# Mixed tile order, sample units dealt out by work, interleaved value products and earlier page loads in a decoder step

## The chip, the cores and the metric

The kernel runs on one core of a Trainium2 chip, as one program launched once. The metric is the device time of one execution in microseconds (us). The core has five engines with a queue each: TensorE (PE, matmuls; its weight loads are shown apart as PEld), VectorE (DVE), ScalarE (ACT), GpSimd (POOL) and SyncE (SP), which here only issues DMAs. Each engine takes its instructions in the order in which they were put down when the program was built, and semaphores make one wait for another.

## The reference

One layer of a hybrid decoder is computed for a prompt of 1024 rows and for a sample group of 8 sequences with 4 rows each, 1056 rows in all, with a width of 1024 and all arithmetic in float32:

- RMS norm with a shift and a scale from a conditioning vector, then one combined projection into gate inputs u and v, 8 query heads, six key/value parts, branch gates and merge gates;
- mixer A: v is normalised, mixed in time within chunks of 128 rows by a lower-triangular matrix, and multiplied by u;
- mixer B: attention with three branches. Compressed: each block of 64 rows is pressed by a small two-layer network into one key and one value, and a softmax goes over these. Selected: a softmax over the 16 best blocks of 64 rows. Window: a softmax over the last 512 rows. Sigmoid gates weigh and add the three;
- both mixers go through a projection, are gated, added, projected and added to x;
- a feed-forward part with a causal convolution of width 3, and a last RMS norm.

The sample sequences have a past of 8192 rows each, in 64 pages of 128 rows that a page table names. The compressed branch reads all pages' compression rows, and the selected branch's keys and values lie in the same pages:

```python
kc = compress_blocks(rows[:, :, :, 0], cmp_pe[0], cmp_w1[0], ...)
p_cmp = masked_softmax(jnp.einsum('btkgd,bnkd->btkgn', qg, kc), avail)
_, sel_idx = lax.top_k(imp, n_sel)
s = jnp.einsum('qkgd,qksid->qkgsi', qi, kg)
...
s = jnp.einsum('bnqkgd,bnjkd->bnqkgj', qg, kw[:, :, :, 0])
o_win = jnp.einsum('bnqkgj,bnjkd->bnqkgd', p, kw[:, :, :, 1])
```

## The kernel before

The program is written stage by stage. A recording layer gives each instruction its place in its engine's queue: it goes through the program with estimated durations and lets an instruction that is ready go ahead of an earlier one that is not. So the order in a queue is near the order of the code but not the same, and it is fixed once the program is built.

Projections are kept feature by row: 128 features by 1056 rows in three column pieces of 384, 384 and 288 (`products`, line 396). Each float32 product is made of three matmuls on a high and a low part of its operands. All matmuls but transposes go through the helper `mm` on line 55, so the profile shows most of them under that line. `slot()` hands out one of 24 buffers of 128 by 1056; PSUM tiles come from four small pools (`pA` with 3 banks for scores, `pT`, `pO`, `pU`).

The compression of the sample pages is cut into 16 parts (`compress`, line 517, and `compress_end`, line 531). Part n loads 32 page tiles of 128 KB into one buffer, does 64 matmuls on it, then an activation and two small products. There is one such buffer, and from part 9 on a second one for odd parts, so the pages of the next part can be loaded when the matmuls of the last one in that buffer are done. `load_pages` (line 491) issues the loads in groups of four; of eight groups in a row it gives those numbered 1, 4 and 6 to ScalarE's queue and the others to SP's. The parts are dealt over the projections: parts 5 to 8 lie behind the four u projections, parts 9 to 13 behind groups of four further projections, and parts 14 and 15 come after the last merge gates, the loads of the queries and the building of key tiles (`key_tiles`, line 733).

The attention stage holds two kinds of work that have nothing to do with each other until its end:

- 32 prompt units: 8 tiles of 128 query rows, each with 4 pairs of heads. `attend` (line 1054) makes scores, maxima, exponentials and scalings of a unit; `combine` (line 1112) transposes the probabilities and multiplies them by the values, two units later (`AHEAD`). Tile i sees i + 1 key tiles in the selected branch and up to 5 in the window branch, so a unit of tile 7 has several times the work of one of tile 0. At the start of a tile `qtile` (line 1004) makes its split queries and the compressed branch.
- the sample group: two windows (`sample_window`, line 861), each for four sequences; 32 sample units, a quarter of a sequence's selected pages each, with scores (`sel_scores`), a transposition called the turn (`sel_turn`) and value products (`sel_values`); after each fourth unit a merge (`sel_merge`). A unit loads 16 page tiles of 128 KB into one of four buffers, which it shares with the windows and with eight late chunks of the conditioning product (`ada_late`).

The loop at line 1162 deals the second kind over the first: iteration n attends unit n, combines unit n - 2 and does sample unit n - 2. The tiles run in the order of `TILES` on line 24.

In a sample window the value products multiply, for each of four sequences i, four pieces k of 128 window rows, and a last piece with the four new rows. The output of sequence i goes to partitions 32i to 32i + 31, that is to the i-th group of 32 columns of TensorE's array; the profile shows such a matmul as 128*32 (rows by columns of the stationary tile).

Of the kernel before, what the change touches and what calls it, by code (L numbers as in the profile page):

```python
# [20 lines left out]
AHEAD = 2  # L21
S2, S3 = 4, 2
EARLY = 8
TILES = (0, 1, 2, 3, 4, 5, 6, 7)
YP = (0, 1, 3, 5, 7), (2, 5)
VD = (0, 2, 4, 6, 8)
SCALE = {1: "dppd", 2: "ppddppdd"}
# [22 lines left out]
def step_kernel(tc, A):  # L50
# [3 lines left out]
    def mm(out, lhsT, rhs, start, stop):  # L54
        return pe.matmul(out, lhsT, rhs, start=start, stop=stop)  # L55
# [17 lines left out]
    def pU():  # L73
        return psum([128, 512], F32, "U", 2)
# [440 lines left out]

    hidden = {}

    def compress(n):
        b, half = n // 2, n % 2
        home = "b" if n >= LATE and n % 2 else "a"  # L520
        st = (R2B if home == "b" else PG)([128, 32, 256], F32, "st", 1)
        load_pages([(st[:, i], A["pcmp"], b * 64 + half * 32 + i) for i in range(32)], freed.get(home))
        ps = pU()
        for d in range(32):
            for s in range(2):
                mm(ps[64 * s:64 * s + 64, 0:128], w1(d, s),
                   st[:, :, s * 128 + 4 * d:s * 128 + 4 * d + 4], d == 0, d == 31)
        hidden[n] = ps, home
# [194 lines left out]
    for n in range(9, 14):  # L723
        for _ in range(4):
            next(fill)()
        compress(n)
        compress_end(n)
    for f in fill:
        f()
    for b in range(8):  # L730
# [130 lines left out]
    def sample_window(gr):  # L861
# [30 lines left out]
        pe.transpose(pt[0:32, 0:128], s[:, 512:544], ident)  # L892
        dve.tensor_copy(pst[0:32, 512:640], pt[0:32, 0:128])
        po = pU()
        for i in range(4):
            v = wv[:, i]
            for k in range(4):
                mm(po[32 * i:32 * i + 32, 0:128], pst[:, 128 * k + 32 * i:128 * k + 32 * i + 32], v[:, k], k == 0, False)
            mm(po[32 * i:32 * i + 32, 0:128], pst[0:32, 512 + 32 * i:544 + 32 * i], vs_new[:, 128:256], False, True)
        ow = R3([128, 128], F32, "ou", 5)  # L900
        uses[use] = act.copy(ow, po[:, 0:128])
# [247 lines left out]
    def sel_first(m):  # L1149
        if 0 < m <= 32:  # L1150
            turned[m - 1] = sel_turn(m - 1, held[m - 1][2])
        if 0 <= m < 32:
            held[m] = sel_scores(m)

    def sel_second(m):
        if 0 < m <= 32:
            use, st, _ = held.pop(m - 1)
            sel_values(m - 1, use, st, turned.pop(m - 1))
            if m % 4 == 0:
                sel_merge(m // 4 - 1)  # L1160

    for n in range(len(units) + AHEAD + 1):
        attend_n(n)
        if n < 2:
            sample_window(n)
        sel_first(n - 2)
        combine_n(n - AHEAD)
        sel_second(n - 2)
        if n % 4 == 1 and n < 32:
            ada_late()  # L1170

# [337 lines left out]
```

## Time and profile before

| what | value |
|---|---|
| time, median of 3 runs | 2093.46 us (2092.12 to 2093.72) |
| the profiled execution's own time | 2091.29 us |
| its span in the trace | 2089.4 us |
| TensorE busy | 1984.5 us, 95% |
| VectorE busy | 992.5 us, 48% |
| ScalarE busy | 748.0 us, 36% |
| GpSimd busy | 314.6 us, 15% |
| read from HBM | 264.57 MB |

The busy times say how long an engine had something in work, not whether it worked at its best. TensorE's clock has two levels, 2.4 and 1.2 GHz, and the profile gives the granted share of it for each stretch: 1.00 is the upper level throughout, 0.50 the lower. Where one matmul of a group goes through other columns of the array than the next one, their records lie over each other in time, so a group's length is read from the first start to the last end.

### The profile page before, as it was taken

To read this page: it belongs to the slowest core of one execution; us is meant where nothing else is said; L and a number is where in the kernel's file an instruction comes from. 1 tells how busy PE (TensorE), PEld (TensorE's weight loads), DVE (VectorE), ACT (ScalarE), POOL (GpSimd) and SP (SyncE) were. 2 spreads that over 40 slices of the span, in tenths; PEclk is the share of its full clock that TensorE was granted. 3 is DMA by queue.
4 is the path that set the end of the run, shared out by engine and by line. 5 is a ranking of instruction groups with operands and counts; after the bars stand their busy time and mean duration, and the time that the engine had idled before them with its cause. 6 is when DMAs were issued, how large, how long until landed. Compare 5 with 4: busy or idle time off the path is not lost.

```text
span 2089.4 us, 41176 instructions
## 1 busy us (share of the span) xinstructions
PE 1984.5 (95%) x15449; PEld 1813.2 (87%) x15449; DVE 992.5 (48%) x2273; ACT 748.0 (36%) x1598; POOL 314.6 (15%) x506
## 2 busy tenths in 40 slices
PE   5889899999998999999999999999999999999996
PEld 3889899999996566666669999999999999999995
DVE  6512521111125476667663767545353453453466
ACT  3311211212123455556562356541331422413433
POOL 3410010100001132222330500210110100101102
PEclk7999999999996899999999999999999999999998
DMA  8465577655464787757531634121221111111112
GB/s 309 137 201 156 180 223 249 218 163 163 144 221 145 222 254 244 256 155 240 166 107 65 237 116 141 52 70 56 66 66 46 45 47 46 46 46 46 40 50 84
DMA packets 217671, 288.35 MB, mean 138 GB/s; under 512 B 25504, under 2 KB 170048, under 8 KB 215296
## 3 DMA queue, kind: packets, MB, share of 16 engines
q1 hardware_dynamic: 155152, 207.88, 31.0%
q10 hardware_dynamic: 57040, 59.58, 9.0%
q0 software_dynamic: 5280, 18.26, 2.4%
q8 instruction: 122, 2.00, 0.4%
q14 instruction: 77, 0.63, 0.1%
HBM read 264.57 MB, written 25.21 MB: 139 GB/s over the span
## 4 chain that ended last, share of the span: by engine, by line
PE 85%; DVE 7%; DMA 4%; ACT 2%; issue 1%; SPq 1%; ACTq 0%; DVEq 0%
PE t L55 81%; PE t L1122 3%; DMA t<-pcmp 2%; DVE t L1085 1%; PE t L939 1%; DMA t<-psel 1%; DVE t L1110 1%; SPq L512 1%; DVE t L1394 1%; DVE t L307 1%; DVE t L766 0%; DMA t<-xT 0%; DMA t<-w_bb 0%; ACT t L306 0%; DVE t L1253 0%
## 5 line engine op out<-in xcount | busy, mean ns | idle before, releaser
L55 PE MATMUL t<-t,t 128*128 128x384 f32 (+12 forms) x14738 | 1899.9, 319 | 72.7 <-DVE t L159 14.7
L55 PEld LDWEIGHTS t<-t,t 128*128 128x128 f32 (+2 forms) x14610 | 1729.8, 169 | 194.2 <-issue 92.2
L307 DVE TENSOR_TENSOR t<-t,t 128x512 fp32r<-128x512 f32 (+5 forms) x322 | 240.8, 755 | 439.3 <-ACT t L306 436.2
L306 ACT CAST t<-t 128x512 fp32r<-128x512 f32 (+5 forms) x322 | 205.2, 646 | 421.2 <-PE t L55 311.4
L1110 POOL TENSOR_SCALAR t<-t,t 128x384 f32<-128x384 f32 (+3 forms) x96 | 118.5, 1247 | 356.5 <-DVE t L1104 94.5
L1237 DVE SCALAR_TENSOR_TENSOR t<-t,t,t 128x384 f32<-128x384 f32 (+1 forms) x168 | 95.9, 572 | 111.0 <-PE t L55 110.3
L1086 ACT ACTIVATE t<-t,t 128x384 f32<-128x384 f32 (+3 forms) x192 | 105.7, 554 | 55.3 <-DVE t L1085 30.5
L1085 DVE TENSOR_REDUCE t<-t 128x1 f32<-128x384 f32 (+3 forms) x192 | 96.6, 516 | 46.9 <-PE t L55 45.7
L1306 ACT COPY t<-t 128x384 f32<-128x384 f32 x132 | 58.6, 444 | 142.1 <-PE t L55 142.1
L1125 ACT COPY t<-t 128x512 f32<-128x512 f32 (+1 forms) x136 | 76.7, 575 | 56.4 <-PE t L1122 46.3
L1122 PE MATMUL t<-t,t 128*128 128x128 f32 x528 | 90.2, 293 | 0.0
L1315 POOL COPY t<-t 128x2 f32<-128x2 f32 x44 | 19.0, 431 | 435.4 <-ACT t L1306 435.4
L1320 DVE SCALAR_TENSOR_TENSOR t<-t,t,t 128x1072 f32<-128x1072 f32 x44 | 58.7, 1335 | 53.6 <-ACT t L1319 53.6
L1122 PEld LDWEIGHTS t<-t,t 128*128 128x128 f32 x528 | 59.7, 146 | 27.0 <-issue 22.6
L662 ACT ACTIVATE t<-t 128x384 f32<-128x384 f32 (+1 forms) x48 | 22.3, 465 | 133.1 <-PE t L55 98.4
L1319 ACT ACTIVATE t<-t,t 128x1072 f32<-128x1072 f32 x44 | 56.5, 1285 | 28.6 <-DVE t L1308 27.7
L1321 DVE SCALAR_TENSOR_TENSOR t<-t,t,t 128x1072 f32<-128x1072 f32 x44 | 58.7, 1334 | 1.4
L539 DVE TENSOR_SCALAR t<-t,t 128x64 f32<-128x64 f32 x16 | 4.5, 283 | 95.0 <-PE t L55 94.8
L1110 DVE TENSOR_SCALAR t<-t,t 128x384 f32<-128x384 f32 (+3 forms) x96 | 48.9, 562 | 0.3
L534 ACT ACTIVATE t<-t,t 128x128 f32<-128x128 f32 x16 | 7.8, 490 | 101.8 <-PE t L55 96.4
L1300 POOL MEMSET t<- 128x2 f32 x44 | 4.3, 99 | 253.7 <-DVE t L1321 156.1
L1225 POOL TENSOR_TENSOR t<-t,t 128x384 f32<-128x384 f32 (+1 forms) x24 | 28.0, 1173 | 83.2 <-DVE t L1224 81.1
(259 smaller groups left out, 963.9 us busy)
## 6 DMA issues: line engine op xcount, KB each, us to landing
t<-psel SPq DMA_DIRECT2D x384, 128.0 KB
t<-pcmp SPq DMA_DIRECT2D x320, 128.0 KB
t<-pcmp ACTq DMA_DIRECT2D x192, 128.0 KB
t<-w_up SPq DMA_DIRECT2D x88, 256.0 KB
t<-psel ACTq DMA_DIRECT2D x128, 128.0 KB
t<-w_ada SPq DMA_DIRECT2D x16, 1024.0 KB
t<-t SPq DMA_DIRECT2D x28, 528.0 KB
t<-w_t ACTq DMA_DIRECT2D x52, 256.0 KB
```

The source lines that it names most:

```text
L55: return pe.matmul(out, lhsT, rhs, start=start, stop=stop)
L306: act.copy(hi, t)
L307: dve.tensor_tensor(lo, t, hi.bitcast(F32), op=OP.subtract)
L1085: dve.tensor_reduce(nm, bk, axis=AX.X, op=OP.max, negate=True)
L1086: act.activation(P[:, w:w + n], bk, AF.Exp, bias=nm, accum_out=s8[:, branch, h, c:c + 1])
L1110: (dve if e == "d" else pool).tensor_scalar(P, P, fc, None, op0=OP.mult)
L1122: pe.transpose(pt[:, 256 * a + 128 * h:256 * a + 128 * h + 128], P[:, c:c + 128], ident)
L1125: act.copy(pp[:, 0:n], pt[:, 0:n])
L1237: dve.scalar_tensor_tensor(x[:, a:e], ps[:, 0:e - a], gate[:, f, 0:1], base[:, a:e], op0=OP.mult, op1=OP.add)
L1306: act.copy(up[:, 2 + a:2 + e], ps[:, 0:e - a])
L1320: dve.scalar_tensor_tensor(acc[:, 0:w], up[:, 1:1 + w], cw[:, n, 1:2], acc[:, 0:w], op0=OP.mult, op1=OP.add)
L1321: dve.scalar_tensor_tensor(acc[:, 0:w], up[:, 2:2 + w], cw[:, n, 2:3], acc[:, 0:w], op0=OP.mult, op1=OP.add)
```

## The change

Five things are altered.

- The order of the prompt's tiles becomes 4, 5, 1, 6, 0, 7, 2, 3.
- Each prompt unit gets a weight, `i + 1 + min(i + 1, 5) + 6` for tile i. The 33 sample steps are dealt to the iterations in proportion to the summed weights; none to the first two, and three to the third. An iteration can have no sample step, one or several. Of several, the first unit's scores come ahead of the combination, the others behind it.
- In a sample window the value products run over the pieces k outside and the sequences i inside, with the four products of the new rows at the end.
- The page loads of compression parts 14 and 15 are written ahead of the last merge gates and of the key tiles, in a function `compress_load` of their own.
- The page loads of part 5 all go to SP's queue.

```diff
-TILES = (0, 1, 2, 3, 4, 5, 6, 7)
+TILES = (4, 5, 1, 6, 0, 7, 2, 3)
...
+    paged = {}
+
+    def compress_load(n):
         b, half = n // 2, n % 2
         home = "b" if n >= LATE and n % 2 else "a"
         st = (R2B if home == "b" else PG)([128, 32, 256], F32, "st", 1)
-        load_pages([(st[:, i], A["pcmp"], b * 64 + half * 32 + i) for i in range(32)], freed.get(home))
+        load_pages([(st[:, i], A["pcmp"], b * 64 + half * 32 + i) for i in range(32)], freed.get(home),
+                   () if n == 5 else (1, 4, 6))
+        paged[n] = st, home
+
+    def compress(n):
+        if n not in paged:
+            compress_load(n)
+        st, home = paged.pop(n)
...
+    for n in (14, 15):
+        compress_load(n)
     for f in fill:
         f()
...
         po = pU()
+        for k in range(4):
+            for i in range(4):
+                mm(po[32 * i:32 * i + 32, 0:128], pst[:, 128 * k + 32 * i:128 * k + 32 * i + 32], wv[:, i, k], k == 0, False)
         for i in range(4):
-            v = wv[:, i]
-            for k in range(4):
-                mm(po[32 * i:32 * i + 32, 0:128], pst[:, 128 * k + 32 * i:128 * k + 32 * i + 32], v[:, k], k == 0, False)
             mm(po[32 * i:32 * i + 32, 0:128], pst[0:32, 512 + 32 * i:544 + 32 * i], vs_new[:, 128:256], False, True)
...
+    work = [i + 1 + min(i + 1, 5) + 6 for i, _ in units]
+    due = [33 * sum(work[0:n + 1]) // sum(work) for n in range(len(units))] + [33] * (AHEAD + 1)
+    m = 0
     for n in range(len(units) + AHEAD + 1):
         attend_n(n)
         if n < 2:
             sample_window(n)
-        sel_first(n - 2)
+            due[n] = 0
+        mine = range(m, due[n])
+        m = max(m, due[n])
+        for k in mine[0:1]:
+            sel_first(k)
         combine_n(n - AHEAD)
-        sel_second(n - 2)
+        for k in mine:
+            if k > mine[0]:
+                sel_first(k)
+            sel_second(k)
```

The built programs can be compared row by row; such a row has the line, the operation, the tile written, the tiles read and the shape of what is written. Three places follow.

On TensorE, the value products of the first sample window, before. `t755_7736` is the output in PSUM, `t747_7701` holds the window's values, `t752_7726` the turned probabilities and `t171_605` the new rows:

```order
L889 MATMUL t753_7727<-t1_69,t749_7716 128x128 x4
L892 MATMUL t754_7733<-t1_69,t749_7716 32x128
L55 MATMUL t757_7759<-t1_69,t708_7571 128x128
L55 MATMUL t755_7736<-t747_7701,t752_7726 32x128 x4
L55 MATMUL t755_7736<-t171_605,t752_7726 32x128
L55 MATMUL t755_7736<-t747_7701,t752_7726 32x128 x4
L55 MATMUL t755_7736<-t171_605,t752_7726 32x128
L55 MATMUL t755_7736<-t747_7701,t752_7726 32x128 x4
L55 MATMUL t755_7736<-t171_605,t752_7726 32x128
L55 MATMUL t755_7736<-t747_7701,t752_7726 32x128 x4
L55 MATMUL t755_7736<-t171_605,t752_7726 32x128
L55 MATMUL t768_7799<-t769_7800,t413_4101 32x512 x4
```

The same place in the changed program, where the tiles have other numbers:

```order
L900 MATMUL t759_7759<-t1_69,t755_7748 128x128 x4
L903 MATMUL t760_7765<-t1_69,t755_7748 32x128
L55 MATMUL t763_7791<-t1_69,t708_7571 128x128
L55 MATMUL t761_7768<-t753_7733,t758_7758 32x128 x16
L55 MATMUL t761_7768<-t171_605,t758_7758 32x128 x4
L55 MATMUL t780_7863<-t781_7864,t413_4101 32x512 x4
```

The sixteen products now follow each other with the sequence changing at each step, and the four products of the new rows come behind them; what stands ahead and behind is the same.

On VectorE, the key tiles (lines 749 to 751, which are 760 to 762 in the changed program) and the two evictions of compression part 14 (lines 539 and 544, now 548 and 553), before:

```order
L749 TENSOR_TENSOR t_7091<-t_7092,t_7089 64x1024
L750 CAST t_7089<-t_7089 64x1024
L751 CAST t_7090<-t_7090 64x1024
L751 CAST t_7091<-t_7091 64x1024
L812 COPY t_7504<-t_7513 128x4
L539 TENSOR_SCALAR t_606<-t_7310,t_577 128x64
L544 TENSOR_TENSOR t_607<-t_7314,t_580 64x128
```

and in the changed program:

```order
L760 TENSOR_TENSOR t_7301<-t_7302,t_7299 64x1024
L761 CAST t_7299<-t_7299 64x1024
L823 COPY t_7504<-t_7513 128x4
L762 CAST t_7300<-t_7300 64x1024
L548 TENSOR_SCALAR t_606<-t_7415,t_577 128x64
L553 TENSOR_TENSOR t_607<-t_7419,t_580 64x128
L762 CAST t_7301<-t_7301 64x1024
```

One of the two casts of the first key tile has moved behind the evictions.

On TensorE, the first attention scores behind compression part 15 (the rows with 16 matmuls), before, with tile 0:

```order
L55 MATMUL t_7423<-t_7318,t_566 64x128 x16
L55 MATMUL t_7667<-t_7088,t_7120 128x128
L55 MATMUL t_7667<-t_7090,t_7120 128x128
L55 LDWEIGHTS t_72
L55 MATMUL t_7667<-t_76,t_72 128x128
L55 MATMUL t_7673<-t_7089,t_7120 128x128
L55 MATMUL t_7673<-t_7091,t_7120 128x128
```

and in the changed program, with tile 4:

```order
L55 MATMUL t_7423<-t_6984,t_566 64x128 x16
L55 MATMUL t_7667<-t_7298,t_7330 128x384
L55 MATMUL t_7667<-t_7300,t_7330 128x384
L55 MATMUL t_7672<-t_7298,t_7330 128x256
L55 MATMUL t_7672<-t_7300,t_7330 128x256
L55 LDWEIGHTS t_72
L55 MATMUL t_7672<-t_76,t_72 128x128
```

Each head's scores now come in two pieces of 384 and 256 columns instead of one of 128, with one mask (the product with `t_72`) for both.

## Rows read from the trace of the kernel before

**Rows 1.** From the page: the engines' totals, and two rows of the span in 40 equal slices of 52.2 us, TensorE's busy share and its granted clock, in tenths.

```profile
PE 1984.5 (95%) x15449; PEld 1813.2 (87%) x15449; DVE 992.5 (48%) x2273; ACT 748.0 (36%) x1598; POOL 314.6 (15%) x506
...
PE   5889899999998999999999999999999999999996
...
PEclk7999999999996899999999999999999999999998
```

**Rows 2.** Busy time of each engine in stretches of the attention stage: start and end in us, length, then busy us and instructions of PE, PEld, DVE, ACT and POOL, TensorE's granted clock, the DMA engines' busy share and GB/s.

```profile
637.00:668.00 31.00, 21.48 (x203) 15.92 (x202) 22.96 (x104) 14.69 (x59) 6.96 (x10) 0.69 0.65 213
668.00:698.00 30.00, 25.65 (x138) 15.09 (x138) 3.59 (x12) 2.59 (x7) 0.00 (x0) 0.63 0.30 88
698.00:800.00 102.00, 96.25 (x970) 62.41 (x971) 72.91 (x208) 57.74 (x171) 27.20 (x20) 0.95 0.82 260
800.00:915.00 115.00, 109.64 (x1118) 72.82 (x1117) 71.70 (x218) 64.22 (x190) 26.71 (x22) 0.97 0.72 224
915.00:1010.00 95.00, 94.09 (x957) 63.51 (x957) 65.88 (x190) 58.70 (x173) 29.90 (x24) 1.00 0.66 205
1010.00:1103.00 93.00, 85.41 (x829) 58.92 (x826) 61.19 (x173) 59.03 (x147) 27.76 (x20) 0.98 0.44 146
```

**Rows 3.** What TensorE waited for from 698 to 1103 us: the waiting line, what released it, us in total, number of waits, the longest. There are 13 such rows, of 19.2 us.

```profile
PE t L55 <- DVE t L985: 3.1, 3, 1.7
PE t L1029 <- DVE t L1027: 2.8, 2, 2.6
PE t L55 <- DVE t L976: 2.4, 1, 2.4
PE t L55 <- ACT t L306: 2.2, 1, 2.2
...
PE t L939 <- ACT t L932: 1.6, 3, 0.7
...
PE t L55 <- DVE t L944: 1.5, 1, 1.5
...
PE t L55 <- DMA t<-psel: 0.6, 1, 0.6
PE t L943 <- DVE t L988: 0.4, 1, 0.4
...
PE t L55 <- DVE t L929: 0.2, 1, 0.2
```

**Rows 4.** The same from 637 to 698 us, the longest row.

```profile
PE t L889 <- DVE t L885: 5.1, 2, 3.1
```

**Rows 5.** Busy time in three short stretches, columns as in rows 2: the value products of sample window 0, of window 1, and of the first sample unit.

```profile
670.79:680.23 9.44, 9.44 (x45) 5.72 (x48) 0.00 (x0) 0.00 (x0) 0.00 (x0) 0.53 0.00 0
687.18:695.37 8.19, 8.19 (x45) 5.22 (x48) 0.00 (x0) 0.00 (x0) 0.00 (x0) 0.62 0.23 65
709.54:710.60 1.06, 1.06 (x37) 0.86 (x30) 1.06 (x4) 0.91 (x4) 0.17 (x1) 1.00 0.62 193
```

**Rows 6.** TensorE's groups of matmuls by shape from 670.7 to 680.2 us: line, operation, stationary tile, moving tile, count, then busy us, mean ns of one, idle us before them.

```profile
L55 PE MATMUL t<-t,t 128*32 128x128 f32 x32 | 7.6, 420 | 0.0
L55 PE MATMUL t<-t,t 32*32 32x128 f32 x8 | 2.3, 382 | 0.0
```

**Rows 7.** VectorE's groups by shape from 636.6 to 668.3 us, columns as in rows 6 with what ended the idle time: maxima (line 1085), query differences (766), scalings (1110) and one of the two small steps (1106).

```profile
L1085 DVE TENSOR_REDUCE t<-t 128x1 f32<-128x128 f32 x16 | 4.4, 281 | 4.0 <-PE t L55 3.8
L1085 DVE TENSOR_REDUCE t<-t 128x1 f32<-128x256 f32 x7 | 2.7, 411 | 0.0
L766 DVE TENSOR_TENSOR t<-t,t 64x128 fp32r<-64x128 f32 x8 | 2.2, 286 | 0.2
L1110 DVE TENSOR_SCALAR t<-t,t 128x128 f32<-128x128 f32 x8 | 2.0, 288 | 0.0
L1106 DVE RECIPROCAL t<-t 128x4 f32<-128x4 f32 x5 | 0.9, 176 | 0.3 <-ACT t L1086 0.2
```

**Rows 8.** Groups of VectorE from 636 to 1103 us, for the wider shapes of the same lines.

```profile
L1085 DVE TENSOR_REDUCE t<-t 128x1 f32<-128x384 f32 x80 | 43.4, 550 | 13.8 <-PE t L55 13.3
...
L1110 DVE TENSOR_SCALAR t<-t,t 128x384 f32<-128x384 f32 x40 | 22.3, 590 | 0.1
...
L1110 DVE TENSOR_SCALAR t<-t,t 128x256 f32<-128x256 f32 x28 | 15.4, 563 | 0.0
```

**Rows 9.** Two stretches, columns as in rows 2: the matmuls of compression part 5, and the 72 matmuls of the last merge gate (48 of 384 columns, 24 of 288).

```profile
254.00:261.20 7.20, 7.20 (x130) 7.03 (x129) 0.00 (x0) 0.47 (x1) 0.00 (x0) 1.00 0.00 0
602.70:614.30 11.60, 11.60 (x75) 11.43 (x73) 1.07 (x3) 1.40 (x3) 0.53 (x1) 1.00 0.72 228
```

**Rows 10.** VectorE in order of time from 622 us: start, us, line, operation, shapes, count.

```profile
624.24 1.41 DVE L751 CAST t<-t 64x1024 fp32r<-64x1024 f32 x2
...
625.75 0.28 DVE L539 TENSOR_SCALAR t<-t,t 128x64 f32<-128x64 f32 x1
```

**Rows 11.** TensorE in order of time from 600 us, with the idle time before a row and what ended it in brackets.

```profile
626.09 11.09 PE L55 MATMUL t<-t,t 128*64 128x128 f32 x137 [3.49 <-DVE t L539]
```

**Rows 12.** SP's queue in order of time from 228 us: the first 14 of the 20 page loads of compression part 5 that it issues.

```profile
231.59 11.76 SPq L512 DMA_DIRECT2D t<-pcmp  x14
```

**Rows 13.** SP's queue from 212 to 219 us: the last page loads of compression part 4.

```profile
212.56 5.89 SPq L512 DMA_DIRECT2D t<-pcmp  x9
```

**Rows 14.** TensorE in order of time from 213 us.

```profile
223.05 4.14 PE L55 MATMUL t<-t,t 128*64 128x128 f32 x48 [5.51 <-DMA t<-w_t]
```

More of the change, by code (lines that the diff above doesn't have):

```diff
@@ L516, in step_kernel @@
     hidden = {}
-    def compress(n):
+    paged = {}
+    def compress_load(n):
         b, half = n // 2, n % 2
```

## The prediction

> **What bounds the kernel now.** I read the page's head first. TensorE is busy for 1984.5 of 2089.4 us, and its granted clock falls in three places only: at the start, in slices 13 and 14 of 40, which is 627 to 731 us, and a little in the last slice [rows 1]. So the kernel is bound by TensorE's work, and a change that does not alter that work can only win idle time, clock, or overlap between matmuls. The second view cuts the run into stretches [rows 2]. From 637 to 1103 us lies the attention stage that the change reorders. In 637 to 668 TensorE works 21.5 of 31 us at a granted clock of 0.69; in 668 to 698 it works 25.7 of 30 at 0.63, while VectorE does 3.6 us and ScalarE 2.6. After 698 TensorE is nearly full (96 of 102, 110 of 115, 94 of 95, 85 of 93 us). The third view, the waits, says what the rest is: after 698 thirteen kinds of wait make 19.2 us, and no kind is over 3.1 [rows 3]; before 698 the longest is for the scaling of a sample window's scores (line 885), 5.1 us in two waits [rows 4]. Every stretch outside the stage keeps its matmuls.
>
> **The change part by part.** All sums are made against the profiled execution, 2091.29 us (a span of 2089.4 with 1.9 around it), which is 2.2 under the median of the three runs.
>
> *Value products of the sample windows.* The same 40 matmul records of each window (32 with 128 rows, 8 with 32 rows) now go through the four column groups in turn instead of finishing one group first. Before, they fill 9.44 us at clock 0.53 and 8.19 us at 0.62, with VectorE and ScalarE at 0.00 in both [rows 5], so nothing runs beside them and all 17.6 us are on the path. In the first window the 32 large ones take 7.6 us and the 8 small ones 2.3 [rows 6]. A sample unit's own value products have the same shape, count and column groups, in the order that the change brings: 32 records in 1.06 us at a granted clock of 1.00 [rows 5]. At half clock that is 2.1 us. The small ones were four pairs at about 0.6 us; one batch of all four I put at 0.6. Window 0 keeps its wait and low clock ahead of it: 2.7 us. Window 1 lies between 2.7 and 1.4 (full clock); I take 2.0. Saved: 17.6 - 4.7 = 12.9 us. Bounds: 0, if the groups still queue for a reason I don't see, and 14.8, if both run at full clock. No transfer becomes late: the first unit's pages are issued before window 0, and those of the next wait for window 0's buffer and so start earlier too.
>
> *Tile 4 first.* The windows hang on a chain of small VectorE steps, and VectorE is busy 23 of 31 us in 637 to 668 [rows 2]. What stands between it and the scaling of window 0 was, by the order and [rows 7]: 16 maxima of 128 columns (4.5 us), 7 of 256 (2.9), 8 and 2 scalings (2.3 and 1.1), 10 small steps (1.8), 8 query differences (2.3): 14.9 us. Now it is 11 maxima of 256 (4.5), 12 of 384 (6.6), 4 scalings of 256 and 4 of 384 (2.3 and 2.4), 14 small steps (2.5): 18.3 [rows 7, 8]. So window 0 comes some 3.4 us later. TensorE does more meanwhile: 27 matmuls of 256 columns, 24 of 384 and 6 masks are 16,900 columns against 10,600 before, and 72 projection matmuls (25,344 columns) took 11.6 us [rows 9], so 6,300 columns are 2.9 us of work done early. I count 0 for the two together; bounds -4 (the wide units also keep the clock up) and +5 (the chain's own latency grows).
>
> *Mixed order and dealt units behind it.* Work is unchanged, so only waits and clock can go. After 698 the waits are 19.2 us; lost clock, length times (1 - granted), is 102 x 0.05 + 115 x 0.03 + 93 x 0.02 = 10.4 [rows 2, 3]. Four kinds belong to sample units and their merges (lines 985, 976, 944, 988: 7.4 us [rows 3]); in the new order merges 0 to 2 stand beside tiles 5, 5 and 6, where before they stood beside tiles 2, 3 and 4. The starts of tiles (line 1027, 2.8), the turns (939, 1.6) and the end of the stage (306, 2.2) stay as they are. I take 5 of the 7.4 and 2 of the clock: -7. Bounds: -29 (all of it) and +22 (each of 32 turns waits the 0.7 us that the longest did).
>
> *Last compression pages ahead of keys.* The loads stand in the same place in SP's and ScalarE's rows as before, since the recording layer had already put them ahead of the key loads. What moves is the two evictions of compression 14, one VectorE cast earlier in the key tiles. TensorE waited 3.49 us for the first of them (line 539), which was queued behind two casts of 0.7 us each (line 751) [rows 10, 11]: -0.7 us; bounds -1.4 and 0.
>
> *Page loads of compression 5 all on SP.* SP issues 32 loads instead of 20, with two stores among them. Compression 5 runs at 254.0 to 261.2 [rows 9], and by the order 21 projection matmuls now stand ahead of it that stood behind: 21 x 0.16 = 3.4 us, so the pages must be there by 257.4. SP alone issued 9 loads in 5.89 us, 0.65 each, the last until 218.45, and TensorE, which had waited for compression 4's pages (its 128*64 matmuls; the row names another transfer that landed with them), went on at 223.05, 4.6 us later [rows 13, 14]. From 231.6 that gives 231.6 + 32 x 0.65 + 4.6 = 257.0: in time, by 0.4 us. At the 0.84 of the stretch in which both queues issued (14 in 11.76 us [rows 12]) it would be 263, 5.7 late. I take 0, with bounds 0 and +6. The Trainium skill (DMA: Bandwidth & Descriptors, "Issuing engines are not separate DMA queues") says that transfers issued from several engines share the same 16 DMA engines, so that a second queue saves issue time alone; by that rule the slower pitch is the shared engines' and not SP's, and the cost is 0.
>
> Sum: 2091.3 - 12.9 + 0 - 7 - 0.7 + 0 = 2070.7, and 2.2 more on the scale of the median: **2073 us**.
>
> **Rivals.**
> *Only the windows pay.* The waits after 698 are spread over thirteen kinds [rows 3], which speaks for a residue that moves and doesn't shrink. 2073 + 7 = 2080.
> *The order fills everything.* Half of the 29 us instead of a quarter: 2073 - 8, and with the start's -4, 2061. For it: TensorE idles under 1 us in 915 to 1010, with wide tiles [rows 2]. Against: tile 0 and tile 1 still come, in between.
> *The clock stays low.* The clock fell while TensorE waited at 637 to 668 and came back inside the long bursts of window products (granted 0.53 and 0.62 over them [rows 5]). With bursts of 2 to 3 us between the same waits it may not come back until the first combine: window 1 at 2.7, and some 4 us of work behind it at twice the time: 2078. The Trainium skill (TensorE: Matmul & The Clock Gate, "HAM oscillation — how this bites in real kernels") tells of just this: short bursts between waits are each run at the lower rate.
> *Pages are late.* In iteration 2 three units follow each other. A unit's 16 pages are 2.1 MB, 8 us at the 260 GB/s of 698 to 800 [rows 2], and of the 405 us after 698, 12.7 per attention unit, the change's own weights give a sample unit 6 parts in 14, some 5 us of TensorE's time. Four units 3 us late each: 2085. Against: four buffers run ahead, and pages cost TensorE 0.6 us in the whole stage before [rows 3].
> *Column groups don't overlap in the windows.* 2073 + 12.9 = 2086. Against: the same shapes do in [rows 5].
> *Turns wait, and it is slower.* A unit's turn (line 939) needs add, maximum and exponential of its scores, behind a wide tile's maxima of 0.55 us each on VectorE [rows 8]. If two or three units per iteration leave too little TensorE work between scores and turn, every unit pays. From 0.65 us per unit (20.6 / 32) the gain is gone; at 0.8, 2073 + 26 = 2099. Against: three waits of 32, 1.6 us in all [rows 3].
>
> **How the numbers follow.** Forecast 0.37, only the windows 0.22, everything filled 0.12, clock low 0.09, pages late 0.09, no overlap 0.03, turns wait 0.08. A difference of 0.2% is 4.2 us, about what a measurement of this kernel can tell from no change. Faster: everything but the last, and of the two near 2085 a fifth less: 0.88; same 0.05; slower 0.07. The range leaves out the slower case and the far end of the best: 2056 to 2088.
>
> **What would show it.** Right: each window's value products in 1.4 to 3 us; the windows' end some 12 us earlier against the end of compression 15; PE's waits after it at 10 to 15 us; no wait ahead of compression 5. Wrong: windows still 8 us long; a wait on the turns or on selected pages in most units; a gap before compression 5 or 8; waits at the stage's end, where the last sample units now stand next to the release of their buffers.

## The result, and the profile after

The changed kernel takes 2080.95 us (median of 4 runs, 2079.78 to 2082.61), the kernel before 2093.59 in the same comparison (4 runs, 2092.12 to 2094.11). The ratio is 0.9941, 95% interval 0.9924 to 0.9959: the interval lies below 1, so the kernel is faster, by some 0.6%, 8 us above the forecast of 2073 and inside the range of 2056 to 2088. The number is that of the rival "only the windows pay" (2080), and the experiments had to say whether its reason holds as well. Measured again in another comparison, the kernel after ("after" from here on) stood at 0.9964 (0.9948 to 0.9981).

The page of the kernel after, with the rows that answer to [rows 1]:

```profile
PE 1966.6 (95%) x15449; PEld 1803.3 (87%) x15449; DVE 992.6 (48%) x2273; ACT 748.1 (36%) x1598; POOL 315.4 (15%) x506
...
PE   5889899999996899999989999999999999999996
...
PEclk7999999999997999999999999999999999999998
```

The matmuls are the same 15449, and TensorE is busy 17.9 us less with them: busy time holds waiting inside a column group and half clock too. In slices 13 and 14 (624 to 728 us) its share is lower than in [rows 1], 6 and 8 tenths, since the products that filled them are shorter and the waits aren't; the granted clock there is 7 and 9 tenths, where it was 6 and 8. The 8 in slice 21 (1040 to 1092 us) is new.

The stretches of the kernel after, columns as in [rows 2]: the value products of window 0 and window 1 (with the two small products ahead of each), from there to the last matmul of the stage, and from there to the first product of the next stage.

```profile
676.40:679.25 2.85, 2.84 (x46) 2.10 (x50) 0.00 (x0) 0.05 (x1) 0.00 (x0) 0.62 0.00 0
685.12:688.13 3.01, 3.00 (x46) 1.95 (x50) 0.00 (x0) 0.15 (x1) 0.00 (x0) 0.55 0.89 278
688.13:1086.80 398.67, 381.80 (x3903) 257.76 (x3902) 269.30 (x793) 237.87 (x684) 108.87 (x88) 0.98 0.67 209
1086.80:1093.38 6.58, 0.01 (x2) 0.00 (x1) 1.57 (x3) 2.68 (x4) 0.00 (x0) 0.61 1.01 403
```

And the same two last stretches in the kernel before:

```profile
695.37:1100.50 405.13, 387.56 (x3890) 258.18 (x3890) 269.60 (x785) 237.58 (x677) 111.57 (x86) 0.97 0.66 210
1100.50:1102.73 2.23, 0.03 (x2) 0.00 (x1) 2.13 (x4) 2.15 (x4) 0.00 (x0) 1.00 0.96 351
```

The rows of [rows 5] begin with the first value product. Without the two small products, which take the first 0.74 and 0.50 us, the windows' value products went from 9.44 and 8.19 us to 2.11 and 2.51. The stretch behind them is 6.5 us shorter; the idle stretch at the end of the stage is 4.4 us longer, and in it the DMA engines are full (1.01, 403 GB/s).

What TensorE waited for from 637 us to 1092 us in the kernel after (line, releaser, us, times, longest), against [rows 3] and [rows 4]:

```profile
PE t L1040 <- DVE t L1038: 6.5, 4, 2.2
PE t L55 <- ACT t L1097: 5.3, 9, 1.3
PE t L900 <- DVE t L896: 5.2, 2, 3.3
PE t L55 <- DVE t L851: 4.2, 1, 4.2
...
PE t L55 <- DVE t L996: 1.3, 1, 1.3
...
PE t L950 <- ACT t L943: 0.2, 1, 0.2
```

The wait ahead of the windows is as before (5.1, now 5.2, line 896). The sample units' merges (line 996) and turns (line 950) hardly wait any more. The starts of tiles (lines 1038 and 1040) do, four times. The wait of 4.2 us is for line 851, in the selection of the sample group's blocks ahead of the windows. It is line 840 of the kernel before:

```profile
PE t L55 <- DVE t L840: 1.5, 1, 1.5
```

What comes ahead of compression 4 varies (its first matmul stands at 224.4 us in one trace of after and at 219.7 in the other). So I read six stretches behind it from each profiled execution. A runs from the first matmul of compression 4 to the end of compression 13, B to the end of compression 15, C to the end of window 1's products, D to the last matmul of the stage, E to the first product of the next stage, F to the end; all in us, each the difference of two times in the trace. The ratio stands beside them.

| kernel | A | B | C | D | E | F | ratio to before |
|---|---|---|---|---|---|---|---|
| before | 367.3 | 45.7 | 59.3 | 405.1 | 2.2 | 986.7 | 1 |
| after | 369.3 | 48.2 | 46.2 | 398.7 | 6.6 | 987.5 | 0.9941 |
| after again (e5) | 370.9 | 48.3 | 48.5 | 396.7 | 6.8 | 987.2 | 0.9964 |
| e1 windows alone | 368.0 | 46.7 | 48.2 | 404.3 | 2.2 | 987.5 | 0.9955 |
| e2 pages not early | 369.8 | 45.7 | 48.1 | 396.3 | 6.6 | 988.0 | 0.9944 |
| e3 part 5 shared | 368.0 | 47.2 | 47.6 | 395.8 | 6.5 | 988.3 | 0.9947 |
| e4 weights first | 372.4 | 47.9 | 48.1 | 396.4 | 1.5 | 982.8 | 0.9907 |
| e6 units one by one | 369.2 | 48.5 | 46.5 | 391.7 | 3.4 | 991.3 | 0.9923 |
| e7 tiles in order | 371.2 | 47.2 | 48.1 | 412.1 | 2.4 | 986.8 | 0.9992 |
| e8 three mended | 368.9 | 44.8 | 48.4 | 396.3 | 1.5 | 982.5 | 0.9892 |
| e9 mended, one by one | 368.4 | 45.8 | 48.6 | 391.4 | 3.4 | 988.8 | 0.9906 |
| e10 units to short tiles | 367.5 | 46.4 | 48.4 | 408.6 | 1.8 | 987.1 | 0.9969 |
| e11 three first | 367.6 | 44.6 | 48.1 | 405.2 | 1.5 | 987.1 | 0.9944 |
| e12 two in wide | 369.5 | 46.8 | 48.7 | 411.8 | 1.5 | 984.2 | 0.9957 |

Before to after, with the mean of both traces of after: A +2.8, B +2.5, C -11.9, D -7.5, E +4.5, F +0.6: -9.0. So the change paid in two stretches, some 19 us, and gave half of it back in three others. Each row is one trace; the six with the dealing and the order of after lie between 395.8 and 398.7 in D.

### The profile page after: what moved, and what is told of

Same layout as the page of the kernel before. It is cut to its first block, busy times and chain, and to the rows that moved or that the text cites. A ratio compares the mean times of both kernels' runs of the same rounds, so it can differ in the third digit from the quotient of the medians.

```text
span 2080.9 us, 41163 instructions
## 1 busy us (share of the span) xinstructions
PE 1966.6 (95%) x15449; PEld 1803.3 (87%) x15449; DVE 992.6 (48%) x2273; ACT 748.1 (36%) x1598; POOL 315.4 (15%) x506
## 4 chain that ended last, share of the span: by engine, by line
PE 84%; DVE 7%; DMA 5%; ACT 2%; issue 1%; SPq 1%; ACTq 0%; POOL 0%; DVEq 0%; POOLq 0%
PE t L55 80%; PE t L1133 3%; DMA t<-pcmp 3%; DVE t L1096 1%; DVE t L1121 1%; SPq L512 1%; PE t L950 1%; DVE t L1416 1%; DMA t<-w_ba 0%; DVE t L307 0%; DMA t<-psel 0%; DMA t<-w_bb 0%; ACT t L1097 0%; DMA t<-w_rows 0%; ACT t L776 0%
## 5 line engine op out<-in xcount | busy, mean ns | idle before, releaser
L55 PE MATMUL t<-t,t 128*128 128x384 f32 (+11 forms) x14738 | 1885.7, 318 | 82.3 <-DVE t L159 14.6
L1121 DVE TENSOR_SCALAR t<-t,t 128x384 f32<-128x384 f32 (+3 forms) x96 | 48.4, 559 | 0.6
```

Source lines behind the costliest of these rows:

```text
L1121: (dve if e == "d" else pool).tensor_scalar(P, P, fc, None, op0=OP.mult)
```

## The experiments

Every experiment was timed in five rounds beside the kernel before on the same chip; intervals are 95%. The first four and the second four ran together, then e9 with e10 and e11 with e12.

**e1: the windows alone.** The kernel before with the change's third part and nothing else:

```
-        for i in range(4):
-            v = wv[:, i]
-            for k in range(4):
+        for k in range(4):
+            for i in range(4):
```

> The kernel before with the window value products in the new order (key tile outer, column group inner) and nothing else. Theory (the windows pay by themselves, the rest of the change nets to about nothing): both windows' products take about 2.8 and 3.0 us as in the kernel after (9.4 and 8.2 before), the time is 2093.6 - 12 = 2081.6 us, level with the kernel after. Rival 1 (the rest of the change brings 6 us of its own): 2087, slower than after by some 6 us, which needs windows that give only 6. Rival 2 (what the windows win is waited away at the next chain of small steps): 2090 or more.

Measured: 0.9955 (0.9940 to 0.9969), 9.4 us of 2090.23. The stretches with the two windows' products in it:

```profile
673.40:676.69 3.29, 3.24 (x46) 2.16 (x50) 0.00 (x0) 0.09 (x1) 0.00 (x0) 0.50 0.00 0
683.40:686.72 3.32, 3.25 (x46) 2.17 (x50) 0.02 (x1) 0.11 (x1) 0.00 (x0) 0.50 0.45 135
```

Both windows run wholly at a granted 0.50, 1.2 GHz. The value products alone take 2.52 us in each (0.8 less than these rows, which hold the two small products too), 5.0 instead of 17.6. C falls by 11.1 us, and the other stretches move by 1 us at most. This one edit is worth as much as the whole change (0.9941 and 0.9964): the other four parts together net to nothing that can be told.

**e2: no early page loads.** From after:

```
-    for n in (14, 15):
-        compress_load(n)
```

> The kernel after without the two early page loads of compressions 14 and 15. Theory (the 30 matmul records of compression 14 that stand ahead of the last merge gate hold back that gate, with it the slots of the queries and keys, and so the key loads, the key casts and the evictions queued behind them): the key loads are issued 1.5 us before the gate's end again instead of 0.3, TensorE waits 3.8 us instead of 5.7 between 590 us and the end of compression 15, and the time falls by 2 to 3 us against after, to about 2078.4. Rival (the 2.6 us that this stretch got longer are the late page or key transfers of one profiled run): unchanged, 2081, with the wait as in after.

Measured: 0.9944 (0.9929 to 0.9958), B 45.7 instead of 48.2. The time alone cannot tell it from after; the trace can, and every later run agrees. B is 47.2 to 48.5 in the six traces with the early loads (mean 47.9) and 44.6 to 46.8 in the eight without (mean 45.8): they cost 2.1 us. SP's queue shows the mechanism, in the kernel before (start, us, line, transfer):

```profile
608.84 3.92 SPq L772 DMA_DIRECT2D t<-t  x4
612.85 0.99 SPq L744 DMA_DIRECT2D t<-o_k  x2
```

and in the kernel after:

```profile
612.09 7.34 SPq L783 DMA_DIRECT2D t<-t  x4
619.51 0.86 SPq L755 DMA_DIRECT2D t<-o_k  x2
```

The last merge gate ends at 614.3 us before and at 619.8 after, and 2.0 us of that are 30 matmul records of compression 14 that now stand ahead of its 72. The key loads (`o_k`) left 1.4 us ahead of that end; now they leave 0.3 ahead of it. In e2 the 30 records stand behind the gate again, and the key loads leave 1.5 us ahead of its end. ScalarE's key casts wait for them, and TensorE waits for the evictions behind those casts, on both engines:

```profile
625.70 2.11 ACT L759 CAST t<-t 64x1024 fp32r<-64x1024 f32 x2 [5.48 <-DMA t<-o_k]
```

```profile
628.37 0.45 PE L55 MATMUL t<-t,t 64*64 64x64 f32 x8 [2.68 <-ACT t L543]
631.85 11.66 PE L55 MATMUL t<-t,t 128*64 128x128 f32 x143 [3.02 <-DVE t L548]
```

Where [rows 11] had one wait of 3.49 us, there are two, 5.7 together.

**e3: compression 5's pages on both queues.** From after:

```
-        load_pages([...], freed.get(home),
-                   () if n == 5 else (1, 4, 6))
+        load_pages([...], freed.get(home))
```

> The kernel after with compression 5's pages shared out over both queues as before. Theory (SP alone issues them late, and the wait of 0.4 us ahead of compression 5 and the two of 0.6 us up to compression 8 come from that): those three waits go and the time falls by 1 to 2 us, to 2079 to 2080. Rival 1 (the waits up to compression 8 come from the matmuls that stand between compressions 7 and 8, which the queue does not change): 0.4 us, not to be told from no change. Rival 2 (both queues share the same engines, and ScalarE's issuing delays its own work): 2081 to 2083.

Measured: 0.9947 (0.9931 to 0.9962), A 368.0 instead of 369.3. Again the time alone doesn't tell it from after, and the traces do: A is 367.3 to 369.5 in the eight traces that share the pages out (mean 368.2) and 369.2 to 372.4 in the six that don't (mean 370.5), 2.3 us. In after TensorE stood ahead of compression 5 and of compression 8:

```profile
259.00 77.94 PE L55 MATMUL t<-t,t 128*64 128x128 f32 x754 [0.37 <-issue]
...
348.85 3.39 PE L55 MATMUL t<-t,t 128*64 128x128 f32 x58 [0.57 <-DMA t<-pcmp]
```

Both waits are gone in e3. Over all traces TensorE is idle 2.1 us of A without the sharing and 0.7 with it, 1.3 of the 2.3 us; the rest is busy time, and no row says why.

**e4: the next stage's first weights ahead of the eight gate rows.** What E waits for is in the chain that ended last in the kernel after, from 1083 us:

```profile
1083.53 9.15 DMA t<-w_ba
...
1092.71 0.63 ACT t L306
...
1093.38 6.67 PE t L55 x24
```

The first weights of the next stage (`w_ba`, 256 KB) are issued at 1083.53 and are there 9.15 us later, because SP had issued eight loads of 528 KB just ahead of them (line 1223, 4.3 MB):

```profile
1078.23 5.21 SPq L1223 DMA_DIRECT2D t<-t  x8
1083.53 12.75 SPq L336 DMA_DIRECT2D t<-w_ba  x8
```

At the 403 GB/s of that stretch 4.3 MB are 10.7 us. The kernel before issued the same eight from 1085.3 us to 1096.4 as their buffers came free, most of them beside matmuls. The edit, on after (the loads are kept in a list by the helper):

```
+    first = [weights(A["w_ba"][m], 4) for m in range(4)]
+    held_by = loads[-1]
     for m in range(8):
         t = slot()
...
-        sync.dma_start(t, sig_d[m])
-        dense(A["w_ba"][m], 4, ah, al, ...)
+        with tc.issue_after(held_by.ins):
+            sync.dma_start(t, sig_d[m])
+        w = first[m] if m < 4 else weights(A["w_ba"][m], 4)
+        for a, b in CH:
+            products(w, ah, al, a, b, ...)
```

> The kernel after with the first four weight pieces of the next stage (w_ba) loaded ahead of the eight gate rows (528 KB each) on SP. Theory (the stage ends on transfers: eight loads issued from 1078.2 run at some 400 GB/s ahead of the first weights, and TensorE stands still for 6.6 us): the wait at the end of the stage falls from 6.6 us to 0 to 2 and the time by 4.5 to 6.5 us, to 2074.5 to 2076.5. Rival 1 (the weights' buffers come free only at 1083, so the loads of the rows start that much later and the first outputs wait for them): 2080 to 2083. Rival 2 (the wait moves behind the first output's products, to the multiplication with the row): 2079 to 2081.

Measured: 0.9907 (0.9887 to 0.9927), and E 1.5, F 982.8:

```profile
1073.00 10.45 SPq L338 DMA_DIRECT2D t<-w_ba  x4
1083.55 3.15 SPq L1228 DMA_DIRECT2D t<-t  x5
```

```profile
1087.50 12.79 PE L55 MATMUL t<-t,t 128*128 128x384 f32 x75 [1.53 <-ACT t L306]
```

Theory confirmed, and it gives more than the 5 us of E: F is 4.7 us shorter as well. In after the 6.6 us of standstill are followed by 2.62 us of matmuls at a granted 0.50, and 58 us later TensorE waits 2.4 us (line 1246); e4 has neither. The late weights aren't the cause of that second wait, though: the kernel before has it too (line 1224), and so have e10 and e11, which have e4's edit (2.5 and 2.7 us, with an F of 987.1). What decides it stays open. The first row below is after's stretch from 1093.38, the second its wait, the third the wait in the kernel before:

```profile
1093.38:1096.00 2.62, 2.62 (x9) 2.62 (x10) 2.54 (x4) 1.79 (x3) 0.00 (x0) 0.50 0.42 104
```

```profile
PE t L55 <- DVE t L1246: 2.4, 1, 2.4
```

```profile
PE t L55 <- DVE t L1224: 2.1, 1, 2.1
```

Rival 1 was half right in its premise: three of the four weight loads do wait for their buffers, until 1082.2 us. But the first leaves at 1073.0, and TensorE's wait is 1.5 us all the same.

**e5: the kernel after again**, beside the next three.

> The kernel after, unchanged, beside the next three on one chip. The first comparison gave 0.9941 of before. Theory: the same again, 0.993 to 0.995, some 2078 if before stands at 2090 here; with the wait of 6.5 us at the end of the stage. Rival (the runs of before and after differ by the page transfers of the first 220 us, which vary from run to run): a ratio nearer to 0.996.

Measured: 0.9964 (0.9948 to 0.9981), the rival's number, with the wait of 6.8 us at the stage's end. The two intervals for after overlap between 0.9948 and 0.9959.

**e6: the units one by one.** From after, the loop of before with the mixed order of tiles:

```
-    work = [i + 1 + min(i + 1, 5) + 6 for i, _ in units]
-    due = [...]
...
+        sel_first(n - 2)
+        combine_n(n - AHEAD)
+        sel_second(n - 2)
```

> The kernel after with the sample units dealt one per iteration as before, and the mixed order of tiles kept. Theory (the two go together: with the mixed order a wide tile and a short tile alternate, and a short iteration with a whole sample unit has too little work around the unit's waits): from the end of window 1 to the last combine some 403 to 406 us instead of 397, the time 5 us above after. Rival 1 (the order alone does it): 397, no difference from after. Rival 2 (the wait at the end of the stage, 6.6 us in after, comes from the dealt units that finish next to it): it goes back to 2 us and the time stays level with after.

**e7: the tiles in rising order**, the units dealt by work:

```
-TILES = (4, 5, 1, 6, 0, 7, 2, 3)
+TILES = (0, 1, 2, 3, 4, 5, 6, 7)
```

> The kernel after with the tiles in rising order as before, and the units dealt by work. Theory (the two go together): from the end of window 1 to the last combine 403 to 406 us instead of 397, the time 3 to 6 us above after. Rival 1 (the dealing alone does it): 397 and no difference. Rival 2 (wide tiles behind the last windows of work are worse: three units of one iteration pile up at the end): over 406, 8 us or more above after.

Measured: e6 0.9923 (0.9897 to 0.9949), e7 0.9992 (0.9975 to 1.0009). The theory for both, that order and dealing go together, falls. D and E of e6, then D and E of e7:

```profile
683.96:1075.69 391.73, 381.48 (x3903) 254.23 (x3902) 263.62 (x772) 234.84 (x680) 108.35 (x88) 1.00 0.65 206
1075.69:1079.09 3.40, 0.00 (x1) 0.00 (x0) 3.20 (x12) 1.98 (x4) 0.00 (x0) 0.50 0.53 168
```

```profile
685.37:1097.49 412.12, 393.64 (x3890) 256.86 (x3890) 273.26 (x785) 238.21 (x677) 110.63 (x86) 0.98 0.65 206
1097.49:1099.91 2.42, 0.02 (x1) 0.02 (x1) 2.32 (x4) 2.21 (x4) 0.00 (x0) 0.99 0.96 357
```

With one unit per iteration the mixed order runs D in 391.7 us at a granted 1.00; the rising order took 405.1 (before) and 404.3 (e1): the order is worth 13 us of D. Dealing by work adds 5 to it in the mixed order (396.7 in e5) and 7 to 8 in the rising one. In D the sign of the dealing is thus the opposite of what the forecast had: it costs. In the mixed order its price shows at the starts of tiles (line 1040, and line 777, which splits a tile's queries), from 695 us on in e5, then in e6:

```profile
PE t L1040 <- DVE t L1038: 5.5, 3, 2.2
PE t L55 <- DVE t L777: 2.3, 2, 1.9
```

```profile
PE t L1040 <- DVE t L1038: 1.2, 1, 1.2
```

These 7.8 us (7.9 in after) against 1.2 are more than the whole 5. Rival 2 of e6 holds in part: without the dealing E is 3.4, but F is 991.3, some 4 us longer, so the end costs the same. Nor does the long wait belong to the dealing alone, since e7 deals as after does and has 2.4; it takes the mixed order too.

**e8: the three mended.** e2, e3 and e4 in one.

> The kernel after with three edits: no early page loads of compressions 14 and 15, compression 5's pages on both queues, and the next stage's first weights ahead of the eight gate rows. Theory (the three stretches where after gave time back are independent): against after 2.5 us from the first, 1.3 to 1.8 from the second, 7 from the third, some 11 us, a ratio of 0.988 to 0.990 of before. Rival (only the last edit shows, since what comes earlier at 640 us waits on later): 7 us, 0.9905, as the third alone.

Measured: 0.9892 (0.9867 to 0.9917), 2067.05 us against 2089.66. A 368.9, B 44.8, E 1.5, F 982.5: each stretch is as the single edits left it, so they add up. This version beats both kernels.

**e9 and e10: e8 with other dealings.** e9 deals one per iteration as e6 does; e10 turns the weights round:

```
-    work = [i + 1 + min(i + 1, 5) + 6 for i, _ in units]
+    work = [27 - (i + 1 + min(i + 1, 5) + 6) for i, _ in units]
```

> The three mended edits of e8 with the sample units dealt one per iteration as before, the mixed order of tiles kept. Theory (dealing by work gives the short tiles fewest units, so that the starts of tiles 0 to 3 stand alone with their VectorE chain; one per iteration covers them): from the end of window 1 to the last combine about 392 us instead of 396.3, no half clock between 700 and 1080 us, and the time 4 to 6 us below e8: 0.986 to 0.9875 of before, some 2062. Rival (the last merge then stands at the end of the stage and waits there, 1 and 2 us, and the next stage's first splits come late): level with e8, 0.989.

> e8 with the weights of the dealing turned round (27 minus the change's weight, so 19 for tile 0 and 8 for tile 7): short tiles get more units, wide ones fewer, and as many iterations get two or none as in e8. Theory (what costs is that the short tiles lack cover): 390 to 393 us from the end of window 1 to the last combine, level with e9, 4 us below e8. Rival (what costs is uneven dealing itself, two units in one iteration or none): 396 or more, level with e8 or above.

Measured: e9 0.9906 (0.9883 to 0.9930), e10 0.9969 (0.9951 to 0.9987). D of e9, and D of e10:

```profile
683.10:1074.51 391.41, 383.34 (x3902) 255.37 (x3902) 263.45 (x772) 233.67 (x680) 108.11 (x88) 0.99 0.66 206
```

```profile
681.56:1090.15 408.59, 389.26 (x3902) 261.78 (x3902) 273.71 (x792) 238.06 (x683) 107.32 (x88) 0.97 0.63 199
```

e9 has the short D that was expected, and its rival's end: the weights' loads now come behind the last merge (the chain has them leave at 1074.58, right behind its last product), E is 3.4 and F 988.8. D, E and F together are 1383.6 us, in e8 1380.3. So once the end is mended, the dealing that costs in D no longer costs in the sum; the two times (0.9906 and 0.9892) can't be told apart. e10's theory falls: giving the short tiles more units makes D 12 us longer than in e8. The waits at the starts of tiles do go, to 1.0 us in all, but the wait for exponentials (line 1096) is 7.1 us, 1.7 in e8:

```profile
PE t L55 <- ACT t L1096: 7.1, 5, 2.5
...
PE t L1039 <- DVE t L1037: 0.6, 2, 0.4
```

So covering the starts of short tiles isn't enough to make a dealing good.

**e11 and e12: one per iteration, but two units ahead.** Both were to keep e9's D with e8's end: e11 takes three units in the third iteration and one in each after it, e12 gains its lead in tiles 6 and 7.

```
+    due = [min(33, n + 1) for n in range(len(units) + AHEAD + 1)]
```

```
+    due = [min(33, max(0, n - 1) + (n >= 14) + (n >= 22)) for n in range(len(units) + AHEAD + 1)]
```

> e9 with the sample units two iterations ahead: three in the third iteration, as in the kernel after, then one in each, so that the last unit is done two iterations before the last combine. Theory (one per iteration makes the body short, 391.4 us from window 1 to the last combine in e9, and the last units beside the stage's end make its end long, waits of 3.4, 1.2 and 0.5 us and half clock behind them; both are to be had): body 390 to 394 us, the wait at the end 0 to 2 us as in e8, some 982.5 us behind it, and a time 4 to 6 us below e8 and e9: 0.985 to 0.987 of before. Rival (what the one-per-iteration dealing wins in the body it wins only by leaving its last merge to the end): the body grows to 396 and the time stays with e8, 0.989.

> e9 with the same lead of two units, gained later: two units in the third iteration of tile 6 and two in the third of tile 7, one in every other. Theory (an uneven dealing costs little where the iteration is a wide one): body 390 to 394 us, end as in e8, 0.985 to 0.987 of before, level with e11. Rival (any iteration with two units costs its 2 to 3 us in waits): body 395 to 398, 0.989 to 0.990.

Measured: e11 0.9944 (0.9925 to 0.9963), e12 0.9957 (0.9939 to 0.9975), both slower than e8, against the theory and beyond the rivals: D 405.2 and 411.8. Both have e8's E (1.5); F is 984.2 in e12 and 987.1 in e11. D of e12:

```profile
686.62:1098.43 411.81, 392.37 (x3902) 258.05 (x3902) 273.83 (x793) 236.85 (x684) 108.14 (x88) 0.97 0.62 198
```

Against e9 TensorE is idle 19.4 us instead of 8.1, in many waits, and busy 392.4 instead of 383.3. The longest wait and what follows it, from 940 us:

```profile
940.35 0.93 PE L55 MATMUL t<-t,t 128*128 128x512 f32 x2 [1.86 <-ACT t L1096]
941.94 3.96 PE L55 MATMUL t<-t,t 128*128 128x512 f32 x12 [0.65 <-ACT t L1096]
949.96 2.50 PE L55 MATMUL t<-t,t 128*128 128x32 f32 x10 [4.06 <-DVE t L995]
```

```profile
940.00:950.00 10.00, 4.93 (x15) 3.12 (x15) 7.33 (x23) 4.10 (x14) 2.98 (x2) 0.54 0.67 209
950.00:964.00 14.00, 13.99 (x125) 7.88 (x125) 3.69 (x9) 5.41 (x14) 2.77 (x3) 0.84 0.32 96
```

A merge (line 995) came just behind the exponentials of a tile, TensorE worked 4.9 of 10 us, and the granted clock was 0.54 there and 0.84 in the 14 us behind. Where the merges stand relative to the tiles changes with every dealing: by VectorE's times (lines 995 and 1037) seven of e11's eight merges begin within 15 us ahead of a tile's start or 7 behind it, in e9 one begins 3 us behind a start and the others keep 15 us or more from the start that follows. That fits e9 and e11. It doesn't explain e12, whose costly merge at 946 us stands 18 us behind a start, nor why after, with its merges 9 to 16 us ahead of most starts, loses only 5. Which rule makes a dealing good stays open.

## Why the prediction was right or wrong

*Value products of the windows: right.* 17.6 us became 4.6 (5.0 in e1), predicted 4.7. The rival that the column groups would still queue is out. The parts were off both ways: window 0 took 2.1 for 2.7, and window 1 took 2.5 for 2.0, since I had taken some of the clock back there and it ran at 0.50 in every trace with the new order. The rival of the low clock had that right (2.7 for window 1), but not the 4 us behind it: from window 1's last product to 690 us the granted clock is 0.81, and over D 0.98. C as a whole fell by 11.9 us, 1.0 less than the forecast. The Trainium skill (TensorE: Matmul & The Clock Gate, "HAM oscillation — how this bites in real kernels") says that a short burst of matmuls behind each wait starts at the low clock, and the trace agrees with it in these two windows.

*Tile 4 first: right.* C is 48.2 and 48.1 us with tile 0 first (e1, e7) and 47.9 as a mean of the eleven with tile 4 first: nothing, as taken. The chain ahead of window 0 did grow: the wait for line 851 (840) is 4.2 us in all eleven and 1.5 in the three with tile 0 first, 2.7 more, where I had the window 3.4 later and 2.9 us of work done meanwhile.

*Mixed order and dealt units: right in the sum, wrong in its parts.* I took -7; D fell by 6.4 and 8.4. That is luck: e6 and e7 show -13 for the order and +5 for the dealing, which I had counted as harmless. The four kinds of wait that I built on did fall, from 7.4 us to 1.3 (line 996). But the starts of tiles, of which I had written that they stay as they are, went from 2.8 to 7.8 and took that back. What is left is busy time, 5.8 us less over D (387.56 to 381.80), where I had 2 for the clock; part of it is clock (0.97 to 0.98), and no run shows the rest. The rival "turns wait" named the wrong wait (the turns' are 0.2 us in all); that dealing two or three units into an iteration costs more of D than it hides is nevertheless what happened, at the starts of tiles.

*Compression 14's evictions: wrong.* -0.7 was forecast with bounds of -1.4 and 0, and it was +2.1. The step that failed is "What moves is the two evictions of compression 14": on TensorE 30 of its 128 records move too, ahead of the last merge gate, and the sum has no term for that. It delays the gate, the buffers that the gate frees, the query and key loads that want them, and the casts ahead of the evictions.

*Compression 5 on one queue: the working right, the term not.* I put the pages at 0.4 us in time; TensorE stood idle for 0.37 us ahead of them, for a reason that the row doesn't name, and for 0.3 to 0.9 in four of the other five traces with the single queue. In the kernel after the first 22 loads of the 32 left in 13.97 us, 0.63 each, where I had taken 0.65:

```profile
233.37 13.97 SPq L512 DMA_DIRECT2D t<-pcmp  x22
...
254.00 1.21 SPq L512 DMA_DIRECT2D t<-pcmp  x2
```

The whole of A is nevertheless 2.3 us longer, through compression 8 as well, which lies between the 0 that I took and the bound of 6. The rule that I weighed there (the Trainium skill, DMA: Bandwidth & Descriptors, "Issuing engines are not separate DMA queues") says that a second queue saves issue time alone, and I let it speak for a cost of 0. The traces don't contradict the rule, but they do my use of it: issue time counted here. The last load had left by 255.2 us where in before it had by 247.9, and sharing them out again (e3) brought the time back.

*The end of the stage: missed.* I wrote that its wait (2.2 us) stays, and listed it only among the signs of being wrong. It is the largest single miss: +4.5 in E. (The 4.7 us that e4 wins behind it were lost in the kernel before as well, whose F is 986.7.) In before the wait's releaser was ScalarE's cast (line 306 [rows 3]), and the chain that ended last leads from there to VectorE and ScalarE, not to a transfer:

```profile
1099.80 1.27 DVE t L307
...
1101.09 1.60 ACT t L306 x2
```

But the DMA engines were already 0.96 busy in that row. I gave no price to the buffers of the eight gate rows coming free earlier and close together, which sends all eight loads out ahead of the first weights.

Stretch by stretch against the forecast, the traces lost 2.8 us in A (2.3 of it by e3's comparison compression 5), 3.2 in B (compression 14), 1.0 in C, 4.5 in E and 0.6 in F, and won 0.5 in D: 11.6 us, between the forecast's sum of -20.6 and the -9.0 of the traces. The range held all this, in part because the two errors inside D cancel.

*Only the windows pay* gave the right number for a reason that is true only of the net: e1 equals after, but the order of tiles pays 13 us in D, and dealing, late weights, early pages and the single queue take them back.

## What to carry to other kernels

An order of work that wins 13 us in its own stretch can be cancelled by small edits that came with it; time each part alone before judging the whole, and read the stretches, since parts of 2 us are below what the time alone tells. When matmuls move ahead of others, price the buffers that those others free and the loads that wait for them. Follow a wait past the cast that released it to the transfer behind the cast, and have the first weights of the next stage issued ahead of whatever large loads that stage wants later.

## What the runs showed that I had not expected

Eight loads of 528 KB issued together run at 403 GB/s with the DMA engines' share at 1.01, and a load of 256 KB issued behind them took 9.15 us to land. How units of work are dealt over iterations is very sensitive: five dealings of the same work over the same tiles gave 391, 396, 405, 409 and 412 us for the stretch.
